# Loading the second half of the first tile from ScalarE's queue in a DMA-bound masked softmax

## Chip, cores and metric

The kernel runs on one core of one Trainium2 chip. The metric is the time of one execution on the device in microseconds, as the median of several executions; "span" is the part of one profiled execution that the profile covers. All runs quoted here are with a granted clock of 1.0.

## The reference

A softmax over the last axis of a float32 tensor of 16 x 8 x 256 x 256, where each of the 16 batches has its own length. Columns beyond the length are zero in the result.

```python
for b in range(batch):
    length = lengths[b]                      # drawn from 128 to 255
    masked = x[b, :, :, :length].copy()
    masked = masked - np.max(masked, axis=-1, keepdims=True)
    exp_masked = np.exp(masked)
    result[b, :, :, :length] = exp_masked / np.sum(exp_masked, axis=-1, keepdims=True)
```

## The kernel before

One batch is one tile: 2048 rows as 128 partitions x 16 rows x 256 columns, 2 MB. Eight slots in on-chip memory hold tiles. SyncE's queue loads tiles 0 to 3 whole; GpSimd's queue loads tiles 4 to 15, each only as wide as its length needs. All stores go through SyncE's queue. For each tile VectorE masks (the lines named L195), ScalarE takes exponentials and row sums, half a tile as one block (L252), and VectorE divides (L219, L222). The parts that matter here:

```python
# loads: ScalarE issues the lengths, SyncE everything up to tile 3
nc.scalar.dma_start(out=word64, in_=lengths[None, :]).then_inc(s_word, 16)
for h in range(2):                                       # tile 0 in two halves
    s = slice(h * half, (h + 1) * half)
    nc.sync.dma_start(out=xt[:, 0, s], in_=x_f[0, :, s]).then_inc(s_ld[h], 16)
for b in range(1, ahead):                                # tiles 1 to 3
    nc.sync.dma_start(out=xt[:, b], in_=x_f[b]).then_inc(s_ld[b + 1], 16)

# stores, in the same queue; the first one waits for three exponential blocks
nc.sync.wait_ge(s_exp, 3)
for b in range(batch):
    for s in parts(b):                                   # parts(0) is the whole tile
        nc.sync.wait_ge(s_out, 2 * b + (s.stop - 1) // half + 1)
        ...                                              # cut
        nc.sync.dma_start(out=out_f[b, :, s, :], in_=xt[:, b % slots, s, :])...

# GpSimd: loads of tiles 4 to 15 start when tile 2 has landed
nc.gpsimd.wait_ge(s_ld[ahead - 1], 16)
...                                                      # cut

# VectorE, in this fixed order
mask(0, slice(0, half))          # waits for half 0
mask(0, slice(half, nt))         # waits for half 1
for b in range(batch):
    first = b == 0 or b >= ahead
    if first:
        divide(b, 0)
    if b + 1 < batch:
        mask(b + 1, slice(0, nt))
    if not first:
        divide(b, 0)
    divide(b, 1)
```

The softmax here doesn't subtract the row's maximum and nothing guards it: scores larger than these inputs give would overflow.

Of the kernel before, what the change touches and what calls it, by code (L numbers as in the profile page):

```python
# [20 lines left out]
def kernel(  # L21
# [6 lines left out]
    nc = tc.nc  # L28
# [9 lines left out]
    x_f = x.rearrange("b h q k -> b (h q) k").rearrange("b (p t) k -> b p t k", p=P)  # L38
# [26 lines left out]
    xt = pool.tile([P, slots, nt, seq_k], F32, name="xt")  # L65
# [15 lines left out]
    with tc.tile_critical(no_gpsimd_drain=True):  # L81
# [4 lines left out]
        s_ld = [sem(f"s_ld{k}") for k in range(ahead + 1)]  # L86
# [17 lines left out]


        nc.scalar.dma_start(out=word64, in_=lengths[None, :]).then_inc(s_word, 16)
        for h in range(2):
            s = slice(h * half, (h + 1) * half)
            nc.sync.dma_start(out=xt[:, 0, s], in_=x_f[0, :, s]).then_inc(s_ld[h], 16)  # L109
        for b in range(1, ahead):  # L110
            nc.sync.dma_start(out=xt[:, b], in_=x_f[b]).then_inc(s_ld[b + 1], 16)  # L111

# [1 line left out]
        for b in range(batch):  # L114
            s_b = s_st[b % 2]
            for s in parts(b):
                nc.sync.wait_ge(s_out, 2 * b + (s.stop - 1) // half + 1)
                if b >= 2 and s.start == 0:
                    nc.sync.wait_ge(s_b, 64 * (b // 2 + 1))
                nc.sync.dma_start(  # L120
                    out=out_f[b, :, s, :], in_=xt[:, b % slots, s, :]
# [48 lines left out]
        def step(ins):  # L170
# [8 lines left out]
                out=down, in0=iota_i, scalar1=0.5, scalar2=-big, op0=ALU.add, op1=ALU.mult  # L179
# [7 lines left out]
                out=len_s, in0=len_f, scalar1=big, scalar2=None, op0=ALU.mult  # L187
# [59 lines left out]
        with nc.Fori(0, 2 * batch, 1, engines=[ACT]) as i:  # L247
            nc.scalar.wait_ge(s_min, i + 1)
            at = bass.ds(i % (2 * slots), 1)
            for j in range(half):  # L250
                e = x_h[:, at, j, :]
                ins = nc.scalar.activation(  # L252
                    out=e, in_=e, func=EXP, accum_out=sum_h[:, bass.ds(i, 1), j]
# [37 lines left out]
```

## Time and profile before

| | |
|---|---|
| time, median of 4 | 156.16 us (155.84 to 156.23) |
| moved by DMA | 62.08 MB, 401 GB/s over a span of 154.7 us |
| busy | VectorE 75%, ScalarE 68%, TensorE 0% |
| tile 0 halves landed | 6.3 and 8.8 us |
| first store issued | 19.86 us |

The DMA engines are busy all the way, so the reading is by stage. The stage view of the kernel before (columns: from:to, length, busy time and count of each engine, granted clock, DMA share, GB/s):

```profile
22.00:24.00 2.00, 0.00 (x0) 0.00 (x0) 1.97 (x3) 2.00 (x11) 0.14 (x1) 1.00 0.92 360
24.00:28.00 4.00, 0.00 (x0) 0.00 (x0) 4.00 (x2) 4.00 (x21) 0.56 (x1) 1.00 0.97 389
```

### The profile page before, as it was taken

To read this page: it belongs to the slowest core of one execution; us is meant where nothing else is said; L and a number is where in the kernel's file an instruction comes from. 1 tells how busy PE (TensorE), PEld (TensorE's weight loads), DVE (VectorE), ACT (ScalarE), POOL (GpSimd) and SP (SyncE) were. 2 spreads that over 40 slices of the span, in tenths; PEclk is the share of its full clock that TensorE was granted. 3 is DMA by queue.
4 is the path that set the end of the run, shared out by engine and by line. 5 is a ranking of instruction groups with operands and counts; after the bars stand their busy time and mean duration, and the time that the engine had idled before them with its cause. 6 is when DMAs were issued, how large, how long until landed. Compare 5 with 4: busy or idle time off the path is not lost.

```text
span 154.7 us, 1324 instructions
## 1 busy us (share of the span) xinstructions
PE 0.2 (0%) x1; PEld 0.1 (0%) x1; DVE 115.7 (75%) x84; ACT 105.2 (68%) x514; POOL 19.0 (12%) x25
## 2 busy tenths in 40 slices
PE   0000000000000000000000000000000000000000
PEld 0000000000000000000000000000000000000000
DVE  1249999952999696979979696969689629796700
ACT  3087799992692959778695959595976906959200
POOL 4910031000220110201111020202001000000000
DMA  4999999999999999999999999999999999999992
GB/s 116 426 449 424 428 398 406 398 407 447 400 410 395 402 409 414 415 417 411 404 424 407 417 408 409 415 416 416 416 417 419 419 448 415 426 445 419 430 421 85
DMA packets 9988, 62.08 MB, mean 401 GB/s; under 512 B 850, under 2 KB 946, under 8 KB 6274
## 3 DMA queue, kind: packets, MB, share of 16 engines
q1 hardware_dynamic: 5904, 41.95, 65.8%
q0 software_dynamic: 4080, 20.12, 32.1%
q14 instruction: 2, 0.02, 0.0%
q10 hardware_dynamic: 2, 0.00, 0.0%
HBM read 28.51 MB, written 33.55 MB: 401 GB/s over the span
## 4 chain that ended last, share of the span: by engine, by line
DMA 55%; DVE 19%; ACT 8%; issue 8%; ACTq 2%; SPq 1%; POOLq 1%; DVEq 0%
DMA xt<-in_x_dram 34%; DMA out_dram<-xt 21%; DVE xt L222 9%; DVE xt L195 9%; ACT xt L252 8%; ACTq L252 2%; DVE inv_sum L219 1%; SPq L109 1%; POOLq L99 0%; SPq L111 0%; SPq L120 0%; DVEq L212 0%; POOLq L135 0%; POOLq L130 0%; ACTq L247 0%
## 5 line engine op out<-in xcount | busy, mean ns | idle before, releaser
L252 ACT ACTIVATE xt<-xt x256 | 102.4, 401 | 37.2 <-DVE xt L195 37.2
L222 DVE TENSOR_TENSOR xt<-xt,inv_sum 128x2048 f32<-128x2048 f32 x32 | 73.4, 2292 | 1.1
L252 ACT ACTIVATION_READ_ACCUMULATOR xt<-xt x256 | 47.9, 187 | 0.0
L195 DVE SCALAR_TENSOR_TENSOR xt<-down,len_s,xt 128x2048 f32<-128x2048 f32 (+1 forms) x17 | 37.8, 2222 | 13.1 <-DMA xt<-in_x_dram 13.0
L130 POOL DMA_DIRECT2D xt<-in_x_dram x12 | 12.8, 1064 | 95.5 <-issue 50.6
L219 DVE RECIPROCAL inv_sum<-row_sum 128x8 f32<-128x8 f32 x32 | 6.3, 198 | 14.4 <-ACT xt L252 14.4
L149 POOL MEMSET xt<- 128x1536 f32 x4 | 5.3, 1386 | 1.1 <-DVE len_s L186 1.1
L244 ACT ACT_TABLE_LOAD x1 | 1.3, 1283 | 1.6 <-SPq L81 1.6
L178 DVE TENSOR_SCALAR down<-iota_i 128x256 f32<-128x256 int32 x1 | 0.3, 297 | 1.6 <-POOL iota_i L141 1.6
L183 DVE CAST len_b<-word 1x16 bf16<-1x16 int32 x1 | 0.2, 163 | 0.4 <-DMA word<-in_lengths_dram 0.4
L186 DVE TENSOR_SCALAR len_s<-len_f 128x16 f32<-128x16 f32 x1 | 0.2, 174 | 0.3 <-PE len_f L165 0.3
L141 POOL IOTA iota_i<- 128x256 int32 x1 | 0.3, 331 | 0.6 <-SPq L81 0.6
L146 POOL MEMSET seed<- 1x1 f32 x2 | 0.3, 162 | 0.0
L244 ACT ACTIVATE warm<-const-float32-0.0 128x1 f32<-128x1 f32 x1 | 0.2, 203 | 0.0
L144 POOL MEMSET ones<- 1x128 bf16 x1 | 0.2, 194 | 0.0
L165 PE MATMUL len_f<-len_b,ones 1*128 1x16 bf16 x1 | 0.2, 164 | 2.6 <-DVE len_b L183 2.6
L275 POOL MEMSET const-float32-0.0<- 128x1 f32 x1 | 0.1, 98 | 0.3 <-issue 0.3
L165 PEld LDWEIGHTS len_f<-len_b,ones 1*128 1x128 bf16 x1 | 0.1, 99 | 2.6 <-POOL ones L144 2.6
L275 POOL MEMSET const-float32-1.0<- 128x1 f32 x1 | 0.1, 98 | 0.0
L275 POOL MEMSET const-bfloat16-1.0<- 128x1 bf16 x1 | 0.1, 98 | 0.0
L275 POOL MEMSET const-uint8-127<- 128x1 uint8 x1 | 0.1, 98 | 0.0
L275 POOL BASE_LOAD x1 | 0.0, 17 | 0.1
## 6 DMA issues: line engine op xcount, KB each, us to landing
out_dram<-xt SPq DMA_DIRECT2D x19, 1024.0 KB
out_dram<-xt SPq DMA_DIRECT2D x14, 512.0 KB
xt<-in_x_dram SPq DMA_DIRECT2D x3, 2048.0 KB, 16.1
out_dram<-xt SPq DMA_DIRECT2D x3, 2048.0 KB
xt<-in_x_dram POOLq DMA_DIRECT2D x3, 1728.0 KB, 16.9
xt<-in_x_dram POOLq DMA_DIRECT2D x2, 2048.0 KB, 18.5
xt<-in_x_dram POOLq DMA_DIRECT2D x2, 1600.0 KB, 16.8
xt<-in_x_dram POOLq DMA_DIRECT2D x2, 1280.0 KB, 14.8
```

Of the source, the lines that this page charges most:

```text
L109: nc.sync.dma_start(out=xt[:, 0, s], in_=x_f[0, :, s]).then_inc(s_ld[h], 16)
L130: nc.gpsimd.dma_start(out=xt[:, slot, :, :w], in_=x_n[:, n, :, :w]).then_inc(s_sw[par], 16)
L141: nc.gpsimd.iota(iota_i, pattern=[[1, seq_k]], base=0, channel_multiplier=0).then_inc(s_iota, 1)
L146: nc.gpsimd.memset(seed[:, par : par + 1], 0.0).then_inc(s_st[par], 64)
L149: nc.gpsimd.memset(xt[:, b, :, low:], 0.0).then_inc(s_fill, 1)
L165: nc.tensor.matmul(len_f, lhsT=ones, rhs=len_b, start=True, stop=True).then_inc(s_lenf, 1)
L195: return nc.vector.scalar_tensor_tensor(out=t, in0=down[:, None, lo:hi].to_broadcast([P, s.stop - s.start, hi - lo]), scalar=len_s[:, b : ...
L219: step(nc.vector.reciprocal(out=inv_sum[:, b, s], in_=row_sum[:, b, s]))
L222: nc.vector.tensor_tensor(out=t, in0=t, in1=inv_sum[:, b, s, None].to_broadcast([P, half, seq_k]), op=ALU.mult,).then_inc(s_out, 1)
L244: nc.scalar.activation(out=warm, in_=nc.const_aps.tensor(0.0, (P, 1), F32), func=EXP)
L252: ins = nc.scalar.activation(out=e, in_=e, func=EXP, accum_out=sum_h[:, bass.ds(i, 1), j])
L275: nc = _bacc.Bacc("TRN2", target_bir_lowering=False, num_devices=1)
```

## The change

Its intent is to let both halves of the first tile be issued at the same time by two engines instead of one after the other, and to free SyncE 0.47 us sooner for tiles 1 to 3.

```diff
         nc.scalar.dma_start(out=word64, in_=lengths[None, :]).then_inc(s_word, 16)
-        for h in range(2):
+        for h, queue in enumerate((nc.sync, nc.scalar)):
             s = slice(h * half, (h + 1) * half)
-            nc.sync.dma_start(out=xt[:, 0, s], in_=x_f[0, :, s]).then_inc(s_ld[h], 16)
+            queue.dma_start(out=xt[:, 0, s], in_=x_f[0, :, s]).then_inc(s_ld[h], 16)
```

## The prediction

> **What bounds the kernel now.** I read the page's slices of the span first, then the DMA share by stage, then the timeline and the chain of waits of the first 40 us, where the change acts, then the landings of the first loads.
>
> From the page: DMA is the mean busy share of the 16 DMA engines in tenths, one digit for each fortieth of the span (3.87 us), and below it the rate.
>
> ```profile
> DVE  1249999952999696979979696969689629796700
> ACT  3087799992692959778695959595976906959200
> ...
> DMA  4999999999999999999999999999999999999992
> GB/s 116 426 449 424 428 398 406 398 407 447 400 410 395 402 409 414 415 417 411 404 424 407 417 408 409 415 416 416 416 417 419 419 448 415 426 445 419 430 421 85
> ```
>
> DMA is at 90% or more in 38 of 40 slices, VectorE and ScalarE are not. The page's total is 62.08 MB; at 416 GB/s that is 149 us of a span of 154.7 us. So transfers bound the kernel nearly from end to end, and only two things can move its end: bytes, which the change leaves alone, or time in which the DMA engines have nothing to do. The stage view (microseconds of the stage, engine times, then DMA share and GB/s at the end of the line) says where such time is:
>
> ```profile
> 0.00:2.00 2.00, 0.00 (x0) 0.00 (x0) 0.30 (x1) 0.36 (x1) 0.91 (x9) 1.00 0.00 0
> 2.00:4.50 2.50, 0.16 (x1) 0.10 (x1) 0.34 (x2) 1.13 (x2) 1.45 (x2) 1.00 0.88 272
> 4.50:24.00 19.50, 0.00 (x0) 0.00 (x0) 14.85 (x12) 13.96 (x69) 5.17 (x4) 1.00 1.01 425
> 24.00:146.00 122.00, 0.00 (x0) 0.00 (x0) 99.55 (x70) 89.74 (x444) 11.48 (x11) 1.00 1.02 416
> ```
>
> Two microseconds pass before the first packet; then 2.5 us run at 272 instead of 425 GB/s, which loses 2.5 x (1 - 272/425) = 0.9 us; from 4.5 us on it is full. The change acts on the first 2.5 us of transfers and on nothing else directly.
>
> The timeline of the first 38 us (start, duration, engine, line, work):
>
> ```profile
> 1.09 0.52 ACTq L106 DMA_DIRECT2D word<-in_lengths_dram  x1
> 1.13 0.86 SPq L109 DMA_DIRECT2D xt<-in_x_dram  x2
> ...
> 2.05 1.91 SPq L111 DMA_DIRECT2D xt<-in_x_dram  x3
> ...
> 6.60 1.28 DVE L195 SCALAR_TENSOR_TENSOR xt<-down,len_s,xt 128x1024 f32<-128x1024 f32 x1 [3.61 <-DMA xt<-in_x_dram]
> 8.15 0.42 ACT L252 ACTIVATE xt<-xt  x1 [5.01 <-DVE xt L195]
> ...
> 9.05 1.29 DVE L195 SCALAR_TENSOR_TENSOR xt<-down,len_s,xt 128x1024 f32<-128x1024 f32 x1 [1.16 <-DMA xt<-in_x_dram]
> ...
> 19.86 8.20 SPq L120 DMA_DIRECT2D out_dram<-xt  x4
> ...
> 20.85 1.29 POOL L130 DMA_DIRECT2D xt<-in_x_dram  x1 [12.46 <-issue]
> ```
>
> (A mask covers 128 columns of 8 rows here, so 128x1024.) SyncE issues the two halves of tile 0 and then tiles 1 to 3; the first mask waits for half 0, the second for half 1, and the first store leaves only at 19.86, because it waits for the third exponential block. The chain of waits of the same stretch puts the single issues at 1.13, 1.58, 2.05 and 2.51, about 0.4 us each with a gap of 0.06, and names what matters later:
>
> ```profile
> 1.13 0.39 SPq L109
> ...
> 1.58 0.42 SPq L109
> ...
> 2.51 16.09 DMA xt<-in_x_dram
> ...
> 20.85 16.54 DMA xt<-in_x_dram
> ...
> 37.62 2.35 DVE xt L195
> ```
>
> The path runs through tile 2's landing at 18.60 (2.51 + 16.09), which lets GpSimd start the later loads, and through tile 4's landing at 37.4, not through tile 0. The landings (issue to landing, min/median/max), for the two halves and for tiles 1 to 3:
>
> ```profile
> DMA to landing us min/median/max: 5.2/6.2/7.2
> ...
> DMA to landing us min/median/max: 11.7/16.1/20.6
> ```
>
> Half 0 landed at 1.13 + 5.2 = 6.3, half 1 at 1.58 + 7.2 = 8.8, tile 1 at 2.05 + 11.7 = 13.7, tile 3 at 3.31 + 20.6 = 23.9 us.
>
> **What the Trainium skill says.** "DMA: Bandwidth & Descriptors", section "Issuing engines are not separate DMA queues": transfers started by different engines run on the same 16 DMA engines and interleave; a second issuer only saves sequencer time. The trace agrees as far as it goes: one queue already fills the engines from 4.5 us on (share 1.01). The same page, "Queues, rings and completion order": each DMA engine takes turns between the queue rows it has work for, packet by packet. No view here shows SyncE's and ScalarE's queues together with work, so I take it from the page. "Perfetto Trace Analysis", "DMA Instruction — HWDGE (DVE, Sync)": the duration of an issue is that of making descriptors, not of moving data. The trace agrees: 0.39 us of issue against 5.2 us to landing.
>
> **The change part by part.**
> 1. *Removed from SyncE*: one issue, 0.42 + 0.05 = 0.47 us. Tiles 1 to 3 are issued 0.47 us sooner. But their packets stand behind tile 0's in queues that are full, so they land when the bytes ahead of them have moved: worth 0 for tile 2's landing at 18.6.
> 2. *Added to ScalarE*: one issue of about 0.42 us after its load of the lengths, so at about 1.66. The table load (1.28 us from 1.64) moves to about 2.1. ScalarE then waits for the first mask till after 8 us: hidden, cost 0.
> 3. *Moved*: half 1's packets now share the engines with half 0's. Issue to first packet was about 1.05 us (1.13 to the first at 2.18 in the packet records), so half 1's first packet comes at about 2.7, not after half 0's last. A tile's half is 1 MB, 8 packets of 8 KB for each engine, each 8192 x 16 / 425 GB/s = 0.31 us. About one packet of half 0 is done by 2.7; the other seven alternate with six or seven of half 1. Estimate: half 0 lands 6.5 x 0.31 = 2.0 us later, at 8.3; half 1, whose last one or two packets now alternate with tile 1's (16 KB, 0.62 us), at 9.1 instead of 8.8.
> 4. *What follows on the engines*: first mask at 8.6 instead of 6.6, ScalarE's first exponential at 10.15 instead of 8.15. Both halves' exponentials then run back to back as now, so everything up to the first store shifts by 2.0: the store's issue from 19.86 to about 21.9, first data near 22.9. VectorE's mask of tile 4 waits 4.42 us for its load, so the 2 us are absorbed there; nothing of it reaches 37.6 through the engines.
> 5. *What follows on the queues*: SyncE's queue holds tile 3 until its engines finish, between 22.5 and 23.6 in the packet records. Today the store stands ready behind it. At 22.9 it comes just as half the engines run dry; GpSimd's first load, issued at 20.85, has its first packet only at 26.5, so it does not fill this hole. Estimate: 0.1 to 0.4 us of idle DMA, on average over the 16 engines 0.2, which a DMA-bound kernel keeps to the end.
> 6. *Gain in the ramp*: a second queue with work may fill the gaps of 2.0 to 4.5 us. At most the 0.9 us worked out above; as the first packets are slow one by one, I choose 0 to 0.3, middle 0.15.
> Sum: 0 - 0.15 + 0.2 = +0.05, plus a little for the uncertain restart at 22.9: I say 156.3 against 156.19.
>
> **The rivals.**
> A. *The parallel issue fills the ramp and shortens the kernel by up to 0.9 us* (155.3). For: 0.88 share and 272 GB/s in that stage. Against: the first transfer alone has 128 packets for 16 engines, so a lack of issued work is not what holds it.
> B. *The late store opens a hole* of 1 us or more, if half 0 lands later than 8.3 or the restart is slow: 157.0 to 157.3. For: no margin left at 22.9 against 22.5 to 23.6. Against: each further 0.1 us costs only 0.1.
> C. *No alternation to speak of*: half 0 keeps its lead, since its packets were queued first; then half 0 lands at about 6.3 to 7 and the store stays before 20.6, hidden: 156.0 to 156.2.
> D. *ScalarE becomes the bound*: 105.2 us busy of 154.7 and one issue of 0.4 us in an idle stretch; excluded.
>
> **Range and chances.** Three runs of before span 155.84 to 156.23. The terms add up to between -0.7 (A) and +1.0 (B); both ends are under 0.7%, a third of 2%, so a verdict other than the same needs something not in this list, such as a different order of loads and stores later on. Predicted 156.3 us, range 155.6 to 157.0; faster 0.01, same 0.98, slower 0.01.
>
> **What would show it.** Step 3: the first mask starts near 8.6 and the second directly after it (before: 6.60 and 9.05); a first mask below 7.2 is rival C. Step 4: first exponential near 10.15, first store issue near 21.9, and VectorE's wait at tile 4 shrunk from 4.42 to about 2.4. Step 1: GpSimd's first load still issued at 20.85 within 0.3. Step 5: DMA share between 22 and 24 us lower than before. Step 6: GB/s between 2.0 and 4.5 us above 272 but below 330. The prediction is wrong if the DMA share falls anywhere after 24 us, or if the end moves by more than 1 us while the stages up to 24 us match.

## The result

| | before | changed |
|---|---|---|
| time, median of 4 | 156.16 us | 157.55 us (157.3 to 158.22) |
| span of the profiled execution | 154.7 us | 156.6 us |
| half 0 / half 1 landed | 6.3 / 8.8 us | 6.4 / 14.0 us |
| first store issued | 19.86 us | 23.75 us |
| KB moved from 22 to 28 us | 2276 | 1504 |

The ratio is 1.010 (95% interval 1.0066 to 1.0134). A ratio here is the mean time of one kernel's fast runs over that of the other's of the same rounds, so it isn't quite the ratio of the medians. The change is within the 2% that counts as the same, but it is clearly longer, and 157.55 lies above the predicted range of 155.6 to 157.0. (The profiled execution, at 158.22, was the slowest of the four.)

The slices of the page of the changed kernel:

```profile
DMA  4999999999999999999999999999999999999991
GB/s 105 427 433 442 419 341 275 407 429 423 397 396 410 410 426 401 419 409 408 414 412 424 401 417 407 410 416 418 418 420 420 429 429 429 425 444 439 412 425 71
```

The DMA digits look as full as before, and that is the trap: the sixth and seventh slice (19.6 to 27.4 us) read 9 and 9 but moved 341 and 275 GB/s, where the kernel before moved 398 and 406. All others but the first and the last agree within 6%. The stage view says the same with sharper edges; it also shows that the start (2 to 4.5 us) won nothing, 252 GB/s against 272:

```profile
2.00:4.50 2.50, 0.17 (x1) 0.10 (x1) 0.34 (x2) 1.49 (x2) 1.42 (x2) 1.00 0.90 252
...
22.00:24.00 2.00, 0.00 (x0) 0.00 (x0) 2.00 (x2) 2.00 (x12) 0.77 (x2) 1.00 0.74 186
24.00:28.00 4.00, 0.00 (x0) 0.00 (x0) 3.93 (x5) 4.00 (x22) 0.00 (x0) 1.00 0.99 283
```

The loss is 2276 (2 x 360 + 4 x 389) - 1504 = 772 KB; at the 417 GB/s of the long stage after it, 772 / 417 = 1.85 us. The span grew by 1.9 us. So the whole loss is made between 22 and 28 us (by the bytes counted in the traces the changed kernel is 1.8 us behind at 28 us and 1.7 at 150), some 14 us after the transfer that was moved should have landed. The timeline shows how one leads to the other:

```profile
1.13 0.39 SPq L109 DMA_DIRECT2D xt<-in_x_dram  x1
...
1.57 1.58 SPq L111 DMA_DIRECT2D xt<-in_x_dram  x3
...
1.66 0.38 ACTq L109 DMA_DIRECT2D xt<-in_x_dram  x1
...
6.65 1.28 DVE L195 SCALAR_TENSOR_TENSOR xt<-down,len_s,xt 128x1024 f32<-128x1024 f32 x1 [3.63 <-DMA xt<-in_x_dram]
14.20 1.28 DVE L195 SCALAR_TENSOR_TENSOR xt<-down,len_s,xt 128x1024 f32<-128x1024 f32 x1 [6.26 <-DMA xt<-in_x_dram]
...
20.91 1.30 POOL L130 DMA_DIRECT2D xt<-in_x_dram  x1 [12.50 <-issue]
...
23.75 0.42 SPq L120 DMA_DIRECT2D out_dram<-xt  x1
```

Half 0 is where it was: first mask at 6.65 (before 6.60). Half 1, issued at 1.66, holds the second mask till 14.20 (before 9.05). VectorE works in a fixed order, so the division of half 0 and the mask of tile 1 wait behind that mask, and the first store is issued at 23.75, after tile 3's last packets (22.5 us in the packet records). GpSimd's first load is where it was, 20.91.

Where half 1 was in the meantime is in the queue view of the changed kernel, first from 2 to 5.5 us, then from 6 to 12 us (q1 is SyncE's queue, q10 ScalarE's; packets, MB, share of the 16 engines):

```profile
q1 hardware_dynamic: 131, 1.07, 94.2%
q10 hardware_dynamic: 2, 0.00, 0.0%
```

```profile
q1 hardware_dynamic: 105, 1.69, 65.6%
q10 hardware_dynamic: 108, 0.88, 34.8%
```

Till 5.5 us ScalarE's queue moved only the two tiny packets of the lengths, though half 1 had been issued almost 4 us before; its first packet starts at 5.77 in the packet records, when half 0 is done. From then on the two queues take turns, packet by packet: 105 against 108. But the packets of tile 1, which now stands in SyncE's queue where half 1 used to be, are 16 KB (a partition's whole row of a tile), and half 1's are 8 KB. So half 1 gets a third of the rate for 8 turns: 8 x (0.31 + 0.61) = 7.4 us, from 5.8 to 13.2, and it landed at 14.0.

### The profile page after: what moved, and what is told of

The parts are those of the page before. It is cut to its first block, busy times and chain, and to the rows that moved or that the text cites. A ratio compares the mean times of both kernels' runs of the same rounds, so it can differ in the third digit from the quotient of the medians.

```text
span 156.6 us, 1324 instructions
## 1 busy us (share of the span) xinstructions
PE 0.2 (0%) x1; PEld 0.1 (0%) x1; DVE 115.3 (74%) x84; ACT 105.2 (67%) x514; POOL 19.0 (12%) x25
## 3 DMA queue, kind: packets, MB, share of 16 engines
q10 hardware_dynamic: 146, 1.05, 1.6%
## 4 chain that ended last, share of the span: by engine, by line
DMA 58%; DVE 16%; issue 8%; ACT 5%; ACTq 1%; POOLq 1%; SPq 1%; DVEq 0%
DMA xt<-in_x_dram 41%; DMA out_dram<-xt 17%; DVE xt L222 8%; DVE xt L195 8%; ACT xt L252 5%; ACTq L252 1%; DVE inv_sum L219 1%; SPq L120 1%; POOLq L99 0%; POOLq L135 0%; POOLq L130 0%; SPq L111 0%; SPq L109 0%; DVEq L212 0%; ACTq L247 0%
## 6 DMA issues: line engine op xcount, KB each, us to landing
xt<-in_x_dram POOLq DMA_DIRECT2D x2, 2048.0 KB, 18.6
```

## The experiments

The theory after the result has two links. First: half 1 is late because it takes turns with tile 1's larger packets. Second: that costs time only because the late first store leaves the DMA engines short of work at 22 us. The rivals: ScalarE's queue is slow by itself; the late engines (VectorE and ScalarE, 4 us behind) cost in some other way; two hardware queues at once cost something. The runs, each in five rounds with the kernel before on the same chip:

| run | half 1 landed | first store issued | KB from 22 to 28 us | time (median) | ratio to before |
|---|---|---|---|---|---|
| kernel before | 8.8 | 19.9 | 2276 | 156.1 | 1 |
| changed kernel, again | 13.8 | 23.6 | 1470 | 157.85 | 1.0104 |
| late_store_before | 8.7 | 22.95 | 1556 | 157.51 | 1.0092 |
| early_store_after | 13.7 | 22.5 | 1576 | 157.54 | 1.0092 |
| act_first | 9.05 | 22.96 | 1578 | 157.64 | 1.0099 |
| half_store_after | 13.7 | 17.8 | 2128 | 156.70 | 1.0044 |
| half_store_before | 8.9 | 14.2 | 2078 | 156.50 | 1.0028 |
| early_load_after | 14.0 | 23.8 | 2172 | 156.31 | 1.0013 |
| early_load_before | 8.8 | 19.8 | 2056 | 156.70 | 1.0027 |
| hold_short | 10.0 | 19.85 | 2322 | 156.06 | 1.0005 |
| split_tile1_before | 8.9 | 20.0 | 2326 | 156.04 | 0.9993 |
| split_tile1 | 11.4 | 21.2 | 2246 | 157.52 | 1.0086 |
| hold_tile1 | 8.8 | 21.0 | 2342 | 157.76 | 1.0108 |

(The landing times are those of the semaphores in the traces; KB are worked out from each run's stage view as above.) With the exception of the last two rows, the time goes with the KB moved in that stage: 2050 KB and more gives 156.0 to 156.7, under 1600 gives 157.5 to 157.9. The 95% intervals of the ratios reach 0.0015 to 0.0035 to either side.

### hold_tile1: tile 1 kept out of the way

```diff
+        nc.sync.wait_ge(s_ld[0], 16)
         for b in range(1, ahead):
             nc.sync.dma_start(out=xt[:, b], in_=x_f[b]).then_inc(s_ld[b + 1], 16)
```

> The changed kernel, but SyncE issues tiles 1 to 3 only after half 0 has landed (about 6.4 us), so that tile 1 has no packets to take turns with half 1. Theory (half 1 was late because its 8 KB packets took turns with tile 1's 16 KB packets, and each engine first works off what it has already taken from SyncE's queue): half 1's first packets come when each engine has finished half 0's eight packets (about 5.2 to 5.7 us) although it was issued at 1.66; half 1 lands at 8.6 to 9.2, the first store is issued at 19.7 to 20.3, the span goes back to that of before: 155.9 to 156.5 us. Rival 1 (half 1 starts only once its turn comes behind tile 1's descriptors, which were made just before its own): without tile 1 it starts at about 2.7, the halves alternate, half 0 lands at about 8.3, the first mask starts at 8.6, the first store near 21.9. Rival 2 (ScalarE's queue is slow by itself): half 1 still lands after 12, 157.5 us.

The queue view of this run, from 2 to 5 us and then from 5.9 to 7.2 us:

```profile
q1 hardware_dynamic: 111, 0.91, 93.1%
q10 hardware_dynamic: 2, 0.00, 0.0%
```

```profile
q10 hardware_dynamic: 66, 0.54, 98.0%
q1 hardware_dynamic: 1, 0.00, 0.0%
```

Half 1 came in one piece directly behind half 0 and landed at 8.8, so ScalarE's queue isn't slow (the expectation's rival 2 is out) and the delay to 14 us is tile 1's doing. Half 1 also didn't alternate with half 0, though nothing else was queued: no data packet of it before 5 us. It had been issued 0.5 us after half 0, and the engines first finished what they had from SyncE. So the expectation's rival 1 is out too.

The time was a miss: 157.76 where 155.9 to 156.5 was expected. Tile 1's packets, issued at 6.39, came too late to follow half 1 without a gap, and tile 1 landed at 14.9 instead of 13.7. In the trace the same number of bytes is reached 0.4 us late at 22 us, 1.0 us late in the middle, and 2.5 us late after a second hole at 140 to 144 us (239 GB/s in that slice of the page, 419 in the kernel before). Why the delay opened that last hole was not pursued. The next form of the experiment removes it.

### hold_short: the same, without the gap

```diff
+        nc.sync.wait_ge(s_fill, 1)
         for b in range(1, ahead):
             nc.sync.dma_start(out=xt[:, b], in_=x_f[b]).then_inc(s_ld[b + 1], 16)
```

> The changed kernel, but SyncE issues tiles 1 to 3 only when GpSimd's first fill is done (about 4.4 us), early enough that the queue doesn't run dry (the longer hold till 6.4 left a gap of about 1 us). Theory (half 1 is late only because it takes turns with tile 1): most of half 1's packets are taken before tile 1's arrive, half 1 lands at 8.6 to 9.8, tile 1 at 13.6 to 14.0, the first store is issued at 19.8 to 20.4, no hole at 22 to 28 us, 155.9 to 156.5 us. Rival (two hardware queues cost something by themselves): half 1 in time, but still over 157 us.

Tile 1 was issued at 4.59. Half 1 landed at 10.0 (a little over the 9.8 expected), tile 1 at 13.7, the first store left at 19.85, and the time is 156.06, a ratio of 1.0005 (0.9983 to 1.0027). The stage view of this run:

```profile
22.00:24.00 2.00, 0.00 (x0) 0.00 (x0) 1.97 (x3) 2.00 (x11) 0.15 (x1) 1.00 0.99 385
24.00:28.00 4.00, 0.00 (x0) 0.00 (x0) 4.00 (x2) 4.00 (x21) 0.56 (x1) 1.00 0.96 388
```

With the moved load kept and SyncE's issues of tiles 1 to 3 held back for 3 us, the whole loss is gone. Two hardware queues by themselves cost nothing that these runs show, and gain nothing.

### split_tile1 and its control: what a turn is worth

```diff
-        for b in range(1, ahead):
+        for h in range(2):
+            s = slice(h * half, (h + 1) * half)
+            nc.sync.dma_start(out=xt[:, 1, s], in_=x_f[1, :, s]).then_inc(s_ld[2], 16)
+        for b in range(2, ahead):
             nc.sync.dma_start(out=xt[:, b], in_=x_f[b]).then_inc(s_ld[b + 1], 16)
...
-                nc.vector.wait_ge(s_ld[b + 1], 16)
+                nc.vector.wait_ge(s_ld[b + 1], 32 if b == 1 else 16)
```

> The changed kernel, with tile 1 loaded in two halves, so that its packets are 8 KB as half 1's are. Theory (the queues take turns by packet, so the sizes of the packets set the shares): half 1 gets one half of the rate instead of one third while both have work, and lands at 10.6 to 11.5 us instead of 13.96; the first store is issued at 20.4 to 21.4, before tile 3's packets end, and the time is 155.9 to 156.6 us. Rival (SyncE's queue has a fixed larger share): half 1 lands at 13 to 14.2 as in the changed kernel, 157.5 us.

> The kernel before with tile 1 loaded in two halves, as the control of the run that split it in the changed kernel (157.5 us, though half 1 landed at 11.4 and no hole was at 22 to 24 us). If the splitting costs by itself: 156.8 to 157.5 us. If it doesn't: 155.9 to 156.4, and the rest of that run's loss comes from its first store leaving at 21.2 instead of 19.9.

The queue view of split_tile1 from 6 to 10 us:

```profile
q10 hardware_dynamic: 109, 0.89, 52.6%
q1 hardware_dynamic: 103, 0.80, 47.5%
```

Again equal numbers of packets, and with equal packet sizes now equal shares: half 1 landed at 11.4 instead of 14.0, as expected. The size of a packet sets what a turn is worth.

The time, again, was a miss: 157.52 where 155.9 to 156.6 was expected, with six executions from 156.82 to 158.21. The control shows that the splitting itself costs nothing (0.9993). The stage from 22 to 28 us was nearly whole (2246 KB); the stage from 28 to 32 us moved 369 GB/s against 421, which is 4 x 52 / 417 = 0.5 us, and by the bytes counted in the trace another 0.4 us were lost between 37 and 51 us. The engines were not idle in the first of these: from 28 to 29.5 us they were busy, but in the packet records SyncE's 16 KB packets took 0.90 us each instead of 0.61. So the store's issue at 21.2 us avoids the hole that one at 22.5 makes, yet something of the delay comes up later. What it is stays open.

### late_store_before: the hole without the change

```diff
-        nc.sync.wait_ge(s_exp, 3)
+        nc.sync.wait_ge(s_exp, 4)
```

> The kernel before with no load touched; only the first store waits for four exponential blocks instead of three and so leaves at about 23.05 us instead of 19.86 (it leaves at 23.75 in the changed kernel). Theory (the loss is the hole that the late first store leaves behind tile 3's last packets at 22.5 us): DMA moves 150 to 250 GB/s between 22 and 24 us instead of 360, and the time is 157.0 to 157.8 us. Rival (the loss comes from the late half 1 in another way, through VectorE and ScalarE or the order of the loads): the time stays at 156.0 to 156.4.

This is the kernel before, with every load as it was; only the first store leaves at 22.95. The stage view:

```profile
22.00:24.00 2.00, 0.00 (x0) 0.00 (x0) 1.97 (x3) 2.00 (x12) 0.59 (x2) 1.00 0.69 154
24.00:28.00 4.00, 0.00 (x0) 0.00 (x0) 4.00 (x2) 4.00 (x22) 0.00 (x0) 1.00 0.98 312
```

The hole is there, 1556 KB, and the time is 157.51, as far up as the changed kernel's. A late first store alone is enough.

### early_store_after: a little earlier is not enough

```diff
-        nc.sync.wait_ge(s_exp, 3)
+        nc.sync.wait_ge(s_exp, 2)
```

> The changed kernel, with the first store waiting for two exponential blocks instead of three, so that it leaves when tile 0 is divided, about 22.6 instead of 23.75 us. Theory of the hole: about 1 us of the hole closes, 156.5 to 157.2 us against 157.5 of the changed kernel. Rival (the late engines matter, not the store): 157.4 to 157.7 as the changed kernel.

The store left at 22.47, 1.3 us sooner, and nothing came of it: 157.54, 1576 KB. This was a miss, and it says that the loss hardly grows with the delay: 1.3 us more of it cost 72 to 106 KB, about 0.2 us. GpSimd's first load had made its descriptors (the orders that the DMA engines work off) by about 22.0, its packets were the only ones there when SyncE's ran out, and the store's first packets came behind them at 26.4 us in the packet records. In the changed kernel they came at 27.4.

### act_first: the alternation that the prediction had assumed

```diff
-        nc.scalar.dma_start(out=word64, in_=lengths[None, :]).then_inc(s_word, 16)
+        nc.gpsimd.dma_start(out=word64, in_=lengths[None, :]).then_inc(s_word, 16)
```

> The changed kernel with the lengths loaded from GpSimd's queue, so that ScalarE issues half 1 at 1.09 us, with SyncE's half 0 and ahead of tile 1. Theory (an engine works off in order what it has taken, and takes from two queues in turn): the halves alternate from the start and both land at 7.9 to 8.8 us, the first mask starts at 8.1 to 9.1; the first store is issued at 21.3 to 22.3, close to the 22.2 us at which GpSimd's descriptors are made, so 156.1 to 157.6 us. Rival (SyncE's queue goes first whatever the order of issue): half 0 at 6.3, half 1 at 9 or later.

With ScalarE free, both halves are issued at 1.09 and 1.14. The timeline:

```profile
9.70 2.48 DVE L195 SCALAR_TENSOR_TENSOR xt<-down,len_s,xt 128x1024 f32<-128x1024 f32 x2 [0.87 <-DMA xt<-in_x_dram]
...
22.96 0.42 SPq L120 DMA_DIRECT2D out_dram<-xt  x1
```

Now the halves did alternate, and landed together at 9.2 and 9.05 (7.9 to 8.8 was expected; the start was slow, 242 GB/s from 2 to 4.5 us). Both masks follow each other at 9.70, the store leaves at 22.96, and the loss is complete: 157.64, at the upper edge of what was expected. The edit changes one thing more: the lengths, now loaded by GpSimd, landed only at 8.12, and VectorE was done with them at 8.83. That is before half 0's landing at 9.23, so they are not what the first mask waited for last, but no run separates the two. So neither order of the two halves gets them both sooner than the single queue did.

### half_store_after and its control: a store in the queue in time

```diff
-            cuts = [0, nt]          # tile 0 stored whole
+            cuts = [0, half, nt]    # tile 0 stored in two halves
...
-        nc.sync.wait_ge(s_exp, 3)
+        nc.sync.wait_ge(s_exp, 1)
```

> The changed kernel with its loads as they are; tile 0 is stored in two halves, the first as soon as it is divided, about 18 us, so that SyncE's queue has 1 MB behind tile 3 before GpSimd's first load has made its descriptors at 22.2 us. Theory (the loss is only that no store stands in SyncE's queue at 22 us): half 1 still lands near 14, but DMA moves over 340 GB/s between 22 and 28 us, and the time is 155.9 to 156.6. Rival (the late half 1 costs by itself, through engines that are 4 us late): 157.2 to 157.7.

> The kernel before with tile 0 stored in two halves, the first at about 14 us instead of both at 19.86. Theory: SyncE's queue already has a store in it at 22 us, so there is no hole to close: 155.9 to 156.4 us. Rival (part of the dips at 22 to 28 us in the kernel before is the same loss): 155.0 to 155.7 us.

With 1 MB of store in SyncE's queue at 17.8 us, half 1 is as late as in the changed kernel and the time is 156.70; the control is 156.50. Both are above the ranges given (156.6 and 156.4) by 0.1 us: an early store costs a little by itself. Its dip is from 22 to 24 us, 238 and 217 GB/s. In the packet records the engines were busy to 96% and 97% from 20.5 to 23 us, but SyncE's 16 KB packets took 0.95 and 1.01 us instead of 0.61; why was not pursued. Between the two, the late half 1 is worth 0.2 us of the 1.4 to 1.8 that the changed kernel loses.

### early_load_after and its control: a load in the queue in time

```diff
-        nc.gpsimd.wait_ge(s_ld[ahead - 1], 16)
+        nc.gpsimd.wait_ge(s_ld[ahead - 2], 16)
```

> The changed kernel again, as the measure for the others of this call: 157.3 to 157.8 us, with the hole at 22 to 28 us.

> The changed kernel, but GpSimd's loads may start when tile 1 has landed instead of tile 2: its first issue moves from 20.9 to about 16 us. Half 1 is as late and the first store leaves as late (about 23.7) as in the changed kernel. Theory (the loss is that between tile 3's last packet and the first packets of the others the DMA engines have nothing): GpSimd's packets now come at about 21.6, while tile 3 is still moving, DMA moves over 300 GB/s between 22 and 24, and most of the loss goes: 156.2 to 157.0 us. Rival (what costs is that the store comes late, or comes after the load, not the emptiness): 157.3 to 157.8.

> The kernel before with the same earlier start of GpSimd's loads, as the control: the queue had no hole, so nothing is gained, 155.8 to 156.5 us; if tile 2 and 3 land later and the engines wait for them, up to 157.

This is the test of the second link from the other side. Half 1 lands at 14.0 and the first store leaves at 23.84, both as late as in the changed kernel; only GpSimd's first load is issued at 16.08, with its first packet at 20.7, while tile 3 is still moving. The stage view:

```profile
22.00:24.00 2.00, 0.00 (x0) 0.00 (x0) 2.00 (x2) 2.00 (x11) 0.00 (x0) 1.00 0.90 340
24.00:28.00 4.00, 0.00 (x0) 0.00 (x0) 3.93 (x5) 4.00 (x21) 0.00 (x0) 1.00 1.08 373
```

2172 KB instead of 1470, and 156.31 instead of 157.85 us: by the ratios (1.0104 and 1.0013) seven eighths of the loss are gone. In the control, where there was no hole to close, the same edit costs 0.27% (its dip of 220 GB/s from 22 to 24 us was not pursued). So the late store and the late engines as such cost little; what costs is that, with no store in SyncE's queue yet, the only work left when its loads run out is a load that GpSimd has just issued.

That is not the same as engines without work. The queue views from 22.5 to 26.5 us show GpSimd's queue (q0), first in the changed kernel, then in this run:

```profile
q0 software_dynamic: 202, 0.97, 88.8%
```

```profile
q0 software_dynamic: 256, 1.23, 89.5%
```

The share of the engines' time is the same, the bytes are not: a packet of 4.8 KB took 0.28 us in the changed kernel (0.888 x 16 engines x 4 us / 202) and 0.22 us here. Beside the stores, from 28 to 32 us of the kernel before, it took 0.19 us. By the packet records the engines of the changed kernel stood idle for 0.56 us each from 22 to 28 us, those of the kernel before and of this run not at all. So about 0.6 of the 1.85 us is emptiness; the other 1.3 us went while the engines were busy with GpSimd's packets alone, which were slow (0.63 us each before 23.5 us). Both parts go when that load starts while tile 3 is still moving. Why its packets are slow otherwise is shown by no run.

No version tried is better than the kernel before; hold_short and split_tile1_before equal it.

## Why the prediction was wrong

- **What bounds the kernel: transfers, right; "only two things can move its end", wrong.** The loss is 1.85 us of missing bytes, but besides bytes and engines with "nothing to do" there was a third thing, engines busy below the full rate: 283 GB/s at a share of 0.99 from 24 to 28 us. So the sign "if the DMA share falls anywhere after 24 us" didn't show (0.97 before), while the rate fell by a quarter.
- **Step 1 (SyncE free sooner, worth 0): right.** Tiles 1 and 2 landed at 13.8 and 18.7, before 13.7 and 18.6; GpSimd's first load left at 20.91.
- **Step 2 (ScalarE hidden): right.** The table load moved from 1.64 to 2.08 and nothing waited for it.
- **Step 3: wrong, the first failure.** "About one packet of half 0 is done by 2.7; the other seven alternate with six or seven of half 1." They didn't: half 1's first packet started at 5.77, after half 0's eight, and alternated with tile 1's instead. The prediction counted one to two turns against tile 1's 16 KB packets; it was eight. Half 0 landed at 6.4 and not 8.3, half 1 at 14.0 and not 9.1. Rival C had the first part of this (half 0 keeps its lead), but drew the wrong end from it, since it didn't ask where half 1 then went.
- **Step 4: the reasoning right, its input wrong.** The shift went through VectorE's order to the store as described, but it was 3.9 us and not 2.0: 23.75 instead of 21.9. The wait for tile 4 took it up, as said: that mask started at 36.8, before 37.6.
- **Step 5: wrong, the second failure, and the one that cost the time.** "0.1 to 0.4 us of idle DMA" and "each further 0.1 us costs only 0.1" (in rival B). The lower share from 22 to 24 us came (0.74 against 0.92), and the idle time itself, 0.56 us, was not far off. What the sum lacked is the 1.3 us in which GpSimd's packets moved slowly. Measured in all: 1.7 to 1.9 us of missing bytes, whether the store was issued at 22.5, 22.95 or 23.75. act_first made step 3's scenario true, with the store at 22.96 instead of the expected 21.9, and had the whole loss: even a right step 3 would not have saved the prediction. The step took the store's first packets to follow 1.05 us after its issue; behind GpSimd's packets it was 3.6 us (from 23.75 to 27.4 in the packet records). And it held GpSimd's load fixed at 26.5, where it stood only because SyncE's packets were ahead of it: in the changed kernel it started at 22.95, alone, slowly at first.
- **Step 6 (gain at the start): wrong in sign, within noise of none.** 252 GB/s in the first profile, 282 in the second, against 272: no gain that can be told from the spread.
- **Rival B** named the late store and the hole, but by another way (half 0 landing late, or a slow restart of the store), and not the slow packets. Its size, 157.0 to 157.3, was nearly right; the range, up to 157.0, left it out.

## What to carry to other kernels

When transfers bound a kernel, a second queue adds no bandwidth but gives away the order: what used to be next in line now shares with whatever stands behind it, in proportion to the size of the packets. Before moving a load, ask which transfer takes its old place, which engine waits for the loser in a fixed order, and whether the first store still is in its queue when the loads run out. Look for such a hole in the GB/s of short stages, not in the busy digits: engines can be busy and slow.

## What the Trainium skill lacked or had wrong

- "DMA: Bandwidth & Descriptors", "Queues, rings and completion order", says that a DMA engine takes turns between queue rows by packet. Once both queues were being served, the trace agrees: 105 against 108 packets. It lacks that a transfer on another queue issued 0.5 us later first waits for what the engines already have: half 1's first packet came 4.1 us after its issue, behind eight packets of half 0 on each engine, also with nothing else queued (hold_tile1). Likewise GpSimd's first load in the kernel before: descriptors made by 22.1, first packet at 26.5, some seven packets of 0.61 us. That engines take packets ahead is inferred from these; how many isn't settled (in early_load_after the same wait was 3.3 us, 17.4 to 20.7).
  Nor does it say what follows for shares: turns are equal, bytes are not. 16 KB against 8 KB packets gave 1.69 against 0.88 MB, 8 KB against 8 KB gave 0.80 against 0.89 MB.
- The same page, "Rules for kernel authors", says that spreading transfers over SP, ACT and GpSimd for bandwidth "Doesn't help". It agrees (no gain here), but it can cost: 1.0% in this kernel, through the order.
- "Perfetto Trace Analysis", "Identifying the Most-Contended Engine", already warns that occupancy misleads for the 16 DMA engines. Here is how far: the share was 0.99 from 24 to 28 us at 283 GB/s, and 0.97 at 389 GB/s in the kernel before.
- No page says that the packets of a load just issued by GpSimd can be slow when they are the only ones: 4.8 KB took 0.63 us before 23.5 us of the changed kernel, against 0.19 us beside stores.
